# A hybrid trunk layer on one core: where the second block's weights are split and kept, when its rotary tables are asked for, and when the weight sums start

## The chip, the cores and the metric

The kernel runs on one core of a Trainium2 chip. The metric is the device time of one execution in microseconds, as the median of the runs shown.

## What is computed

One layer of a decoder trunk on x of 2048 tokens x 1024 columns, all in f32. Cut to what matters:

```python
h = rmsnorm(x, mix_norm_g)
q, k, v, g, u = split(h @ w_in, 5)                # 512 columns each
y_ret = silu(g) * head_rmsnorm(retention(rope(q), rope(k), v))   # 4 heads of 128
y_pool = pool_mixer(u, pool_w) * pool_scale       # trailing means over 2, 4, 8, 16 tokens
x = x + concat(y_ret, y_pool) @ w_out
x = x + softmax(rmsnorm(x, xa_norm_g) @ wq @ k_mem.T / 16) @ v_mem @ wo   # 256 memory tokens, 4 heads
a = rmsnorm(x, ffn_norm_g) @ w_up                 # 2 x 2816 columns
x = x + (silu(conv3(a)[gate]) * conv3(a)[val]) @ w_down
return rmsnorm(x, final_norm_g)
```

## The kernel before

**Blocks and stages.** The tokens are worked in two blocks of 1024 (`T`; b = 0 and 1), each as two halves of 512 (`SUB`). Block 0 goes through its head inputs and retention, its pools, its out-projection and its attention over the memory; then block 1 does the same. The gated MLP comes last, for both blocks, in rounds.

**Matmuls.** Every f32 product is three passes of 128x512 matmuls on parts of reduced precision: high by high (L268), high by low (L269) and low by high (L270). The high part of an operand is a copy on ScalarE (L1118 for a loaded weight, L258 in `split`), the low part the difference on VectorE (L242).

**Seven products instead of eight.** The MLP, and of block 1 also the projections of q, k, g and u, take a 2x2 block product in the form with seven products, which needs sums of weight quarters and sums of the other operand's quarters. `weight_sums` makes the weights' sums in HBM (`Ad` for the pairs of block 1, `Ud` and `Dd` for the MLP) by software DMAs that GpSimd issues, some copying and some adding. It is a generator: one step is a small copy on ScalarE (L1031) that is held in program order, a copy on GpSimd (L1032) behind it, and up to eight DMAs behind that. Between two steps it yields `spacing[0]` times. `under[0]` is advanced by the units of the out-projections and attention's value product while `slow[0]` is false and `paced[0]` true, and elsewhere by a call in the loop. For `VWd` (attention's last product) `under` is set aside for both blocks.

**The start of block 1.** `values` makes v on PE. Beside it `quarter_sums` loads four pieces of x (j = 0 to 3; `R` and `S` hold them, names from the program's buffers), and writes the sums of quarters as split pairs (G) and, for two kinds, unsplit into `z` (Z). Then `head_projections` runs eight members of seven items each, twelve matmuls an item. An item's weight is loaded by SyncE into one of seven places of 512 columns (`raws`, taken as they come free), split into one of four pairs (`prs`), and read by PE; `fill` runs the splits ahead of PE. `turned_sums` splits what `z` holds, `scaled_tables` asks for the rotary tables (`rope_d`, four DMAs into Z) and multiplies them by the norm's factors (VectorE, L242, Z<-Z,T). Both are advanced by `step` between items.

**What sets the order.** A scheduler orders each engine's instructions from the program's text, its buffers and costs; what stands under `tc.keep_in_program_order` keeps the written order on its engine.

**Attention of block 1.** Sixteen iterations (scores and softmax: L969, L973, L946, L948). Beside them `first_tiles` reads block 1's residual back from HBM (T<-Xd), normalises it (L250), and stores it and its quarter sums (Hd<-T). The MLP's first operands are read from there (T<-Hd, split by L1067 on ScalarE).

Of the kernel before, what the change touches and what calls it, by code (L numbers as in the profile page):

```python
# [11 lines left out]
AF = mybir.ActivationFunctionType  # L12
# [5 lines left out]
KT = D // P  # L18
SEQ = 2048
NMEM = 256  # L20
T = 1024
SUB = 512
# [114 lines left out]
def trunk(ctx, tc, xT, memT, pos, w_qkgu, w_v, wkv, wqT, wo, wout_r, wout_p, poolT, w_up, w_dn, vecs, consts, outT):  # L137
    nc = tc.nc
    pe, act, dve, pool, sp = nc.tensor, nc.scalar, nc.vector, nc.gpsimd, nc.sync
# [17 lines left out]
    def new_s(dtype, at):  # L157
        return cp.tile([P, T], dtype, tag=f"S{at}", name=nm("S"))
# [8 lines left out]
    R = cp.tile([P, 3 * T], F32, tag="R", name="R")  # L167
    Q = cp.tile([P, 3 * T], F32R, tag="Q", name="Q")
    S = [new_s(F32, j) for j in range(2)]
    raws = Places([(R, j * T) for j in range(3)] + [(r, 0) for r in S], T)  # L170
# [70 lines left out]
    def tt(eng, out, a, b, op):  # L241
        return eng.tensor_tensor(out=out, in0=a, in1=b, op=op)  # L242

    def ts(eng, out, a, s1, op0, s2=None, op1=None):
        if op1 is None:
            return eng.tensor_scalar(out=out, in0=a, scalar1=s1, scalar2=None, op0=op0)
        return eng.tensor_scalar(out=out, in0=a, scalar1=s1, scalar2=s2, op0=op0, op1=op1)

    def stt(out, a, s, b, op0=ALU.mult, op1=ALU.add):
        dve.scalar_tensor_tensor(out=out, in0=a, scalar=s, in1=b, op0=op0, op1=op1)  # L250
# [50 lines left out]
    def xpair(k, s):  # L301
        return X[:, 2 * k, s * SUB : (s + 1) * SUB], X[:, 2 * k + 1, s * SUB : (s + 1) * SUB]


    quarter, slow, spacing, paced = [0], [True], [4], [False]
    behind, under, fetched = [iter(())], [iter(())], [None]
# [375 lines left out]
    def pool_group(b, g, rb):  # L682
        out = B.take(2)

        def evac(s, ps):
            u, *bufs = [TT.take() for _ in range(3 if g else 2)]
            tt(dve, u.f[:, 16 : 16 + SUB], ps, rb[s].f[:, :SUB], ALU.mult)
            dve.tensor_copy(u.f[:, 0:16], phalo[:, g])
            dve.tensor_copy(phalo[:, g], u.f[:, SUB : SUB + 16])
            src, lo = u, 1  # L690
            for i in range(g + 1):
                sh = 1 << i
                dst = bufs[i % 2]
                tt(dve, dst.f[:, lo : 16 + SUB], src.f[:, lo : 16 + SUB], src.f[:, lo - sh : 16 + SUB - sh], ALU.add)
                src = dst
                lo += 2 * sh
            cur, d = u.f[:, 16 : 16 + SUB], src.f[:, 16 : 16 + SUB]
            w = 2 << g
            if b == 0 and s == 0:
                tt(dve, d[:, :w], d[:, :w], icnt[:, :w], ALU.mult)  # L700
                ts(dve, d[:, w:], d[:, w:], 1.0 / w, ALU.mult)
                tt(dve, d, d, cur, ALU.subtract)
            else:
                stt(d, d, 1.0 / w, cur, ALU.mult, ALU.subtract)
            split(d, out.r[:, s * SUB : (s + 1) * SUB], out.r[:, T + s * SUB : T + (s + 1) * SUB])
            for r in (u, *bufs):
                r.free()

        unit(load_tile(w_qkgu[12 + g]), xpair, evac)
        return out  # L710
# [388 lines left out]
    class Member:  # L1099
# [15 lines left out]
        def high(self, i, pr):  # L1115
            w = self.n * P
            p2 = pr.r.rearrange("p (i n) -> p i n", i=2)
            act.activation(p2[:, 0, :w], self.raw[i].f[:, :w], AF.Copy)  # L1118
            return p2[:, 0, :w], p2[:, 1, :w]
# [437 lines left out]
        return r.r[:, 2 * j * SUB : (2 * j + 1) * SUB], r.r[:, (2 * j + 1) * SUB : (2 * j + 2) * SUB]  # L1557

    def part_of(z, i, j):
        at = (j // 2) * 2 * T + i * T + (j % 2) * SUB  # L1560
        return z.f[:, at : at + SUB]

    def quarter_sums(b, t1, t2, z):
# [31 lines left out]
    def negated(src, hi, lo):  # L1595
        act.activation(hi, src, AF.Copy, scale=-1.0)
        stt(lo, src, -1.0, hi.bitcast(F32), ALU.mult, ALU.subtract)

    def head_projections(b, v, rb, t1, t2, z):
# [2 lines left out]
        nonlocal raws, prs  # L1602
        pieces, far = B.arenas[0], new_e(F32)
        more = new_s(F32R, 0)
        raws = Places([(R, j * SUB) for j in range(5)] + [(S[1], j * SUB) for j in range(2)], SUB)
        side = Arena(R, 5 * SUB, 1, SUB).take().f
        prs = Places([(Q, j * T) for j in range(3)] + [(more, 0)], T)
        t3 = pieces.take(4)
        todo, ready, mix, gates, outs, tables = [], [], [None] * KT, {}, {}, []

        def place():
            return Z.take() if Z.room() else far.take()

        def turned_sums():
            for j in range(KT // 2):
                split(part_of(z, 0, j), *fourth(t3, j))
                yield
            z.free(0, 1)
            z.free(2, 1)
            for j in range(KT // 2):  # L1620
                negated(part_of(z, 1, j), *xpair(j, 1))
                yield
            z.free(1, 1)
            z.free(3, 1)

        def scaled_tables():
            out = Z.take(2)
            tables.append(out)
            for to, half in ((0, 0), (0, 1), (2, 0), (1, 1)):
                p, i = slice(64 * half, 64 * half + 64), min(to, 1)  # L1630
                sp.dma_start(out.f[p, i * T : (i + 1) * T].rearrange("p (s c) -> p s c", s=NS), rope_d[to].rearrange("(s p) c -> p s c", s=NS))
            yield
            yield
            for i in range(2):
                for s in range(NS):
                    d = out.f[:, i * T + s * SUB : i * T + (s + 1) * SUB]
                    tt(dve, d, d, rb[s].f[:, :SUB], ALU.mult)
                yield
# [37 lines left out]
        class Heads(Member):  # L1676
# [6 lines left out]
            def begun(self):  # L1683
                both_gates = self.groups[0] // 4 == 2
                self.acc = []
                for n in self.groups:
                    if n // 4 == 2:
                        gates[n % 4] = None if both_gates else [TT.take() for _ in range(NS)]
                    if n // 4 == 2 and not both_gates:
                        self.acc.append([g.f[:, :SUB] for g in gates[n % 4]])  # L1690
                    else:
                        r = place()
                        self.acc.append([r.f[:, q * SUB : (q + 1) * SUB] for q in range(NS)])
                        outs[n] = r

            def evac(self, i, ps):
                role, q = ((0, 0), (1, 1), (0, 1), (0, 0), (1, 1), (0, 1), (1, 0))[i]
# [95 lines left out]
            if todo and next(todo[0], True) is not None:  # L1793
                todo.pop(0)

        todo += [turned_sums(), scaled_tables()]
        for at, (m, i) in enumerate(items):
            while len(made) <= at or highs:
                fill()
# [3 lines left out]
            pr = made[at].r.rearrange("p (i n) -> p i n", i=2)  # L1803
# [29 lines left out]
        raws = Places([(R, j * T) for j in range(3)] + [(r, 0) for r in S], T)  # L1833
# [72 lines left out]
    todo = folded_weights()  # L1906

    def folded(n):
        for _ in range(n):
            next(todo, None)  # L1910
# [12 lines left out]
    for b in range(NB):  # L1923

        if b == 0:
            rn, rb, last = normed
            v = values(lambda: rn, wv)
            with tc.issue_after(last.ins):
                tabs = list(rope_tables(0))[-1]
            cs = rope_scale(tabs, rb)  # L1930
            per = [(0, 1, 1), (0, 1, 1), (0, 2, 2), (0, 2, 3)]
            mix = []
            for h in range(HEADS):
                qkg = head_inputs(h, rb, cs, lambda i: folded(per[h][i]))
                mix.append(B.take(2))
                behind[0] = retention(b, h, qkg, v, mix[h])
            folded(100)
            pooled = {g: pool_group(b, g, rb) for g in (0, 3, 2, 1)}
            finish()
            cs.free()  # L1940
            mix += [pooled[g] for g in range(4)]
            mix = [(u, [u.r[:, :T], u.r[:, T:]]) for u in mix]
        else:
            t1, t2 = (B.arenas[0].take(4) for _ in range(2))
            v, z = Z.take(4), Z.take(4)
            more_sums = quarter_sums(b, t1, t2, z)
            next(more_sums)

            def between():
                next(behind[0], None)  # L1950
                if next(more_sums, None) is None:
                    next(under[0], None)

            values(lambda: normed[0], wv, between, v)
            for _ in more_sums:
                pass
            finish()
            rb = normed[1]
            mix = head_projections(b, v, rb, t1, t2, z)
        for r in rb:  # L1960
            r.free()
        slow[0], spacing[0] = False, (4, 4)[b]

        xs = [TT.take() for _ in range(NS)]
        ahead = fetch_x(b, 0)
# [39 lines left out]
                r.free()  # L2005

        beside = tables() if b + 1 < NB else first_tiles(own)
        paced[0], spacing[0] = True, (1, 2)[b]
        prob, behind[0] = attention(xs, beside, b + 1)
        spacing[0] = 3  # L2010
        for _ in beside:
            pass
        under, paused = [iter(())], under
        Z = new_z(F32)
        xs = [TT.take() for _ in range(NS)]
        if b + 1 < NB:
# [45 lines left out]
        under = paused  # L2062
# [28 lines left out]
    raws = Places([(R, j * SUB) for j in range(6)] + [(r, j * SUB) for r in S for j in range(2)], SUB)  # L2091
# [114 lines left out]
```

## Time and profile before

| | before |
|---|---|
| median of 3 runs | 2466.07 us (2465.82 to 2468.02) |
| profiled execution | 2467.87 us, span 2466.1 us |
| mean granted TensorE clock | 0.992 |
| busy PE / VectorE / ScalarE / GpSimd | 2417.9 / 1726.2 / 1288.9 / 316.1 us |
| software DMA queue | 86.00 MB, 14.9% of the 16 DMA engines over the span |

Stages of the profiled execution: block 0 to about 660 us, values of block 1 to 702, pair products to about 925, out-projection to about 1010, attention to 1100 with its value product to 1230, and the MLP from there. Rows of a timeline give start, length, engine, line, operation, tile written <- tiles read, and in brackets how long the engine had been idle and who ended that. PE's durations overlap, since matmuls are pipelined: its pace is read from start to start.

### The profile page before, as it was taken

What the parts mean: (1) busy time and instruction counts of PE and PEld (TensorE: products, weight loads), DVE (VectorE), ACT (ScalarE), POOL (GpSimd) and SP (SyncE); (2) the same over time, 40 slices, a digit from 0 to 9 for tenths busy, and PEclk for the clock granted to TensorE, in tenths of its full rate; (3) what the DMA queues carried; (4) which work ended last, traced back from release to release, by engine and by line L of the source; (5) the groups of instructions that cost most, each with busy time, mean ns of one, the idle gap of its engine ahead of it and who ended that gap; (6) DMA issues with size and microseconds to landing.
All of it is one profiled execution on the core that took longest, in us unless ns stands there. A gap on an engine that the chain in (4) does not pass through costs nothing.

```text
span 2466.1 us, 33272 instructions
## 1 busy us (share of the span) xinstructions
PE 2417.9 (98%) x11294; PEld 2019.7 (82%) x11294; DVE 1726.2 (70%) x2917; ACT 1288.9 (52%) x2349; POOL 316.1 (13%) x485
## 2 busy tenths in 40 slices
PE   6999999999989999999999999999999999999997
PEld 6888888888878887878888888888888888888886
DVE  8646576564756665565778776886767698867875
ACT  6333423443435554434655655675555577666663
POOL 1000000054255554200000100020000000000000
PEclk9999999999999999999999999999999999999998
DMA  8133524389899999766568664765556478768951
GB/s 292 45 111 111 160 76 136 124 219 324 250 273 274 260 236 321 197 232 213 171 200 270 208 188 151 234 214 162 160 159 216 132 230 307 246 185 283 344 164 69
DMA packets 263595, 502.35 MB, mean 204 GB/s; under 512 B 28800, under 2 KB 57600, under 8 KB 263424
## 3 DMA queue, kind: packets, MB, share of 16 engines
q1 hardware_dynamic: 201536, 385.90, 47.8%
q0 software_dynamic: 37376, 86.00, 14.9%
q10 hardware_dynamic: 24512, 28.32, 3.3%
q8 instruction: 89, 1.46, 0.2%
q14 instruction: 82, 0.67, 0.1%
HBM read 398.65 MB, written 187.43 MB: 238 GB/s over the span
## 4 chain that ended last, share of the span: by engine, by line
PE 93%; DMA 3%; DVE 3%; issue 1%; ACT 0%; SPq 0%; POOL 0%; POOLq 0%; DVEq 0%; ACTq 0%
PE mm L270 29%; PE mm L268 29%; PE mm L269 29%; DMA T<-Xd 1%; PE aux L808 1%; PE aux L824 1%; PE aux L797 1%; PE aux L268 1%; PE aux L269 1%; PE aux L270 1%; PE aux L826 1%; PE aux L349 1%; DMA Z<-rope_d 1%; DMA T<-xT 0%; DVE T L242 0%
## 5 line engine op out<-in xcount | busy, mean ns | idle before, releaser
L268 PE MATMUL mm<-G,Q 128*128 128x512 f32 (+1 forms) x1745 | 673.4, 386 | 19.8 <-ACT Q L258 11.0
L270 PE MATMUL mm<-G,Q 128*128 128x512 f32 (+1 forms) x1745 | 669.9, 385 | 10.5 <-DVE Q L242 10.4
L269 PE MATMUL mm<-G,Q 128*128 128x512 f32 (+1 forms) x1617 | 621.2, 384 | 0.0
L269 PE MATMUL mm<-G,E 128*128 128x512 f32 x1084 | 421.6, 389 | 0.0
L268 PE MATMUL mm<-G,E 128*128 128x512 f32 x1084 | 420.1, 390 | 0.0
L270 PE MATMUL mm<-G,E 128*128 128x512 f32 x1084 | 419.2, 389 | 0.0
L268 PEld LDWEIGHTS mm<-G,Q 128*128 128x128 f32 x1745 | 332.0, 190 | 84.8 <-ACT Q L258 12.4
L270 PEld LDWEIGHTS mm<-G,Q 128*128 128x128 f32 x1745 | 331.5, 190 | 76.0 <-DVE Q L242 13.2
L269 PEld LDWEIGHTS mm<-G,Q 128*128 128x128 f32 x1617 | 308.0, 191 | 57.1
L242 DVE TENSOR_TENSOR Z<-Z,mm 128x512 f32<-128x512 f32 x296 | 201.4, 681 | 111.7 <-PE mm L270 104.7
L250 DVE SCALAR_TENSOR_TENSOR Z<-Z,vecs 128x1024 f32<-128x1024 f32 x176 | 224.5, 1279 | 50.2 <-ACT Z L1181 45.5
L270 PEld LDWEIGHTS mm<-G,E 128*128 128x128 f32 x1084 | 203.5, 188 | 42.4
L269 PEld LDWEIGHTS mm<-G,E 128*128 128x128 f32 x1084 | 203.5, 188 | 42.2
L268 PEld LDWEIGHTS mm<-G,E 128*128 128x128 f32 x1084 | 203.5, 188 | 42.1 <-ACT Z L1263 0.2
L1118 ACT ACTIVATE E<-R 128x512 fp32r<-128x512 f32 (+1 forms) x165 | 101.5, 615 | 142.3 <-PE mm L269 135.1
L242 DVE TENSOR_TENSOR T<-T 128x512 f32<-128x512 f32 (+3 forms) x220 | 150.5, 688 | 24.3 <-ACT T L411 15.4
L242 DVE TENSOR_TENSOR G<-T,G 128x512 fp32r<-128x512 f32 (+1 forms) x181 | 119.3, 673 | 44.1 <-ACT G L1067 32.8
L242 DVE TENSOR_TENSOR Q<-R,Q 128x512 fp32r<-128x512 f32 x149 | 103.4, 696 | 66.3 <-ACT Q L258 47.1
L1118 ACT ACTIVATE Q<-R 128x512 fp32r<-128x512 f32 (+1 forms) x153 | 94.5, 618 | 85.4 <-PE mm L269 72.2
L1181 ACT ACTIVATE Z<-Z,vecs 128x1024 f32<-128x1024 f32 x88 | 109.1, 1241 | 36.6 <-DVE Z L242 35.6
L1067 ACT ACTIVATE G<-T 128x512 fp32r<-128x512 f32 x157 | 95.7, 624 | 58.1 <-DMA T<-Hd 27.9
L1118 ACT ACTIVATE E<-S 128x512 fp32r<-128x512 f32 (+1 forms) x107 | 65.8, 616 | 105.0 <-PE mm L269 103.4
(338 smaller groups left out, 3776.7 us busy)
## 6 DMA issues: line engine op xcount, KB each, us to landing
T<-Gd SPq DMA_DIRECT2D x168, 256.0 KB, 4.4
Ud<-w_up POOLq DMA_DIRECT2D x132, 256.0 KB, 10.1
Gd<-Z SPq DMA_DIRECT2D x110, 256.0 KB, 2.7
R<-Ud SPq DMA_DIRECT2D x106, 256.0 KB, 2.8
R<-w_up SPq DMA_DIRECT2D x80, 256.0 KB, 3.1
S<-Ud SPq DMA_DIRECT2D x70, 256.0 KB, 2.9
Gd<-T SPq DMA_DIRECT2D x56, 256.0 KB, 3.3
T<-Xd SPq DMA_DIRECT2D x53, 256.0 KB, 4.6
```

The costliest lines, as they stand in the source:

```text
L242: return eng.tensor_tensor(out=out, in0=a, in1=b, op=op)
L250: dve.scalar_tensor_tensor(out=out, in0=a, scalar=s, in1=b, op0=op0, op1=op1)
L268: pe.matmul(ps, lh, rh, start=start, stop=False, skip_group_check=more)
L269: pe.matmul(ps, lh, rl, start=False, stop=False, skip_group_check=more)
L270: latest[0] = pe.matmul(ps, ll, rh, start=False, stop=stop, skip_group_check=more)
L349: pe.matmul(ps[:, t : t + 1], ap, one, start=True, stop=more is None)
L797: pe.matmul(col(sc, c), self.ch(k, c), self.ch(q, c), start=True, stop=True)
L808: pe.matmul(col(self.kv, c), col(self.kn.f, c), self.ch(v, c, h * T), start=True, stop=True)
L824: pe.matmul(col(y, c), col(self.pr.f, c), self.ch(v, c, h * T), start=True, stop=self.cur[c] is None)
L1067: act.activation(hi, x, AF.Copy)
L1118: act.activation(p2[:, 0, :w], self.raw[i].f[:, :w], AF.Copy)
L1181: act.activation(self.c[g].f, a[:, 2:], AF.Identity, bias=cb[:, f : f + 1], scale=cw[2][:, f : f + 1])
```

## The change

The places for the pairs' weights are listed in the order in which the quarter loads came free (`raws.freed`). `part_of` lays `z` out so that the first kind fills its first two slots and the second kind its last two. `turned_sums` now splits the first kind, frees its two slots, asks for the tables, and only then negates the second kind. `Heads` gets a `high` of its own, which is held in ScalarE's program order. The weight sums are advanced from block 0's pools on, with other spacings, no longer beside the values of block 1, and for block 1 no longer set aside for the value product of attention.

```diff
@@ -1557,7 +1557,7 @@
         return r.r[:, 2 * j * SUB : (2 * j + 1) * SUB], r.r[:, (2 * j + 1) * SUB : (2 * j + 2) * SUB]
 
     def part_of(z, i, j):
-        at = (j // 2) * 2 * T + i * T + (j % 2) * SUB
+        at = i * 2 * T + j * SUB
         return z.f[:, at : at + SUB]
 
     def quarter_sums(b, t1, t2, z):
@@ -1602,7 +1602,9 @@
         nonlocal raws, prs
         pieces, far = B.arenas[0], new_e(F32)
         more = new_s(F32R, 0)
-        raws = Places([(R, j * SUB) for j in range(5)] + [(S[1], j * SUB) for j in range(2)], SUB)
+        rooms = [(R, 0), (R, T), (R, 2 * T), None, (S[1], 0)]
+        rooms = [(rooms[i][0], rooms[i][1] + h * SUB) for i in raws.freed for h in range(1 if i == 2 else 2) if i != 3]
+        raws = Places(rooms, SUB)
         side = Arena(R, 5 * SUB, 1, SUB).take().f
         prs = Places([(Q, j * T) for j in range(3)] + [(more, 0)], T)
         t3 = pieces.take(4)
@@ -1615,13 +1617,8 @@
             for j in range(KT // 2):
                 split(part_of(z, 0, j), *fourth(t3, j))
                 yield
-            z.free(0, 1)
-            z.free(2, 1)
-            for j in range(KT // 2):
-                negated(part_of(z, 1, j), *xpair(j, 1))
-                yield
-            z.free(1, 1)
-            z.free(3, 1)
+            z.free(0, 2)
+            yield from scaled_tables()
 
         def scaled_tables():
             out = Z.take(2)
@@ -1631,6 +1628,10 @@
                 sp.dma_start(out.f[p, i * T : (i + 1) * T].rearrange("p (s c) -> p s c", s=NS), rope_d[to].rearrange("(s p) c -> p s c", s=NS))
             yield
             yield
+            for j in range(KT // 2):
+                negated(part_of(z, 1, j), *xpair(j, 1))
+                yield
+            z.free(2, 2)
             for i in range(2):
                 for s in range(NS):
                     d = out.f[:, i * T + s * SUB : i * T + (s + 1) * SUB]
@@ -1693,6 +1694,11 @@
                         self.acc.append([r.f[:, q * SUB : (q + 1) * SUB] for q in range(NS)])
                         outs[n] = r
 
+            def high(self, i, pr):
+                hi, lo = pr.r[:, :SUB], pr.r[:, SUB:]
+                tc.keep_in_program_order(act.activation(hi, self.raw[i].f, AF.Copy))
+                return hi, lo
+
             def evac(self, i, ps):
                 role, q = ((0, 0), (1, 1), (0, 1), (0, 0), (1, 1), (0, 1), (1, 0))[i]
                 d = self.acc[role][q]
@@ -1793,7 +1799,7 @@
             if todo and next(todo[0], True) is not None:
                 todo.pop(0)
 
-        todo += [turned_sums(), scaled_tables()]
+        todo.append(turned_sums())
         for at, (m, i) in enumerate(items):
             while len(made) <= at or highs:
                 fill()
@@ -1935,6 +1941,7 @@
                 mix.append(B.take(2))
                 behind[0] = retention(b, h, qkg, v, mix[h])
             folded(100)
+            slow[0], paced[0], spacing[0] = False, True, 7
             pooled = {g: pool_group(b, g, rb) for g in (0, 3, 2, 1)}
             finish()
             cs.free()
@@ -1948,8 +1955,7 @@
 
             def between():
                 next(behind[0], None)
-                if next(more_sums, None) is None:
-                    next(under[0], None)
+                next(more_sums, None)
 
             values(lambda: normed[0], wv, between, v)
             for _ in more_sums:
@@ -1959,7 +1965,7 @@
             mix = head_projections(b, v, rb, t1, t2, z)
         for r in rb:
             r.free()
-        slow[0], spacing[0] = False, (4, 4)[b]
+        spacing[0] = (7, 6)[b]
 
         xs = [TT.take() for _ in range(NS)]
         ahead = fetch_x(b, 0)
@@ -2005,12 +2011,12 @@
                 r.free()
 
         beside = tables() if b + 1 < NB else first_tiles(own)
-        paced[0], spacing[0] = True, (1, 2)[b]
+        spacing[0] = (1, 3)[b]
         prob, behind[0] = attention(xs, beside, b + 1)
-        spacing[0] = 3
+        spacing[0] = 6
         for _ in beside:
             pass
-        under, paused = [iter(())], under
+        under, paused = [iter(())] if b == 0 else under, under
         Z = new_z(F32)
         xs = [TT.take() for _ in range(NS)]
         if b + 1 < NB:
```

ScalarE, end of the values stage and start of the pairs. The last two L737 evacuate the last two banks of the values, L1596 and L258 split what `z` holds, L1118 are weights' high parts and L1706 the first evacuation of a pair. Before:

```order
L1118 ACTIVATE Q<-R 128x512
L1596 ACTIVATE G<-Z_4490 128x512
L1031 ACTIVATE halo<-consts 128x2
L258 ACTIVATE G<-Z_4490 128x512
L1596 ACTIVATE G<-Z_4490 128x512
L258 ACTIVATE G<-Z_4490 128x512
L1596 ACTIVATE G<-Z_4490 128x512
L1118 ACTIVATE Q<-R 128x512
L258 ACTIVATE G<-Z_4490 128x512
L737 ACTIVATE Z_4490<-mm_5411,rn_5149 128x4x128
L737 ACTIVATE Z_4490<-mm_5412,rn_5149 128x4x128
L1118 ACTIVATE Q<-S_79 128x512
```

After, where the weights' high parts are L1699 and the evacuation is L1712:

```order
L258 ACTIVATE G<-Z_4550 128x512
L1031 ACTIVATE halo<-consts 128x2
L1596 ACTIVATE G<-Z_4550 128x512
L258 ACTIVATE G<-Z_4550 128x512
L1596 ACTIVATE G<-Z_4550 128x512
L258 ACTIVATE G<-Z_4550 128x512
L737 ACTIVATE Z_4550<-mm_5431,rn_5199 128x4x128
L737 ACTIVATE Z_4550<-mm_5432,rn_5199 128x4x128
L1699 ACTIVATE Q<-R 128x512
L1699 ACTIVATE Q<-S_79 128x512 x2
L1699 ACTIVATE S_5484<-R 128x512
L1712 ACTIVATE E_5483<-mm_5504 128x512
```

Before, high parts stand among the splits and ahead of the values' evacuation; after, all stand behind it. A halo copy (L1031) starts a step of the weight sums: one stands among the splits in either order, but before the change three more stand in the twelve rows ahead of these, and after it none.

VectorE, statistics of the last quarter (`sm`, then `rn`), before:

```order
L242 TENSOR_TENSOR sm_5354<-sm_5352 128x8
L242 TENSOR_TENSOR S_5484<-R,S_5484 128x512
L250 SCALAR_TENSOR_TENSOR sm_5354<-sm_5354,sm_5351 128x8
L250 SCALAR_TENSOR_TENSOR sm_5352<-sm_5354,sm_5352 128x8
L242 TENSOR_TENSOR sm_5354<-sm_5352 128x8
L250 SCALAR_TENSOR_TENSOR sm_5354<-sm_5354,sm_5351 128x8
L250 SCALAR_TENSOR_TENSOR sm_5352<-sm_5354,sm_5352 128x8
L1839 COPY rn_5341<-sm_5352 128x8
```

After:

```order
L242 TENSOR_TENSOR sm_5384<-sm_5382 128x8
L250 SCALAR_TENSOR_TENSOR sm_5384<-sm_5384,sm_5381 128x8
L250 SCALAR_TENSOR_TENSOR sm_5382<-sm_5384,sm_5382 128x8
L242 TENSOR_TENSOR sm_5384<-sm_5382 128x8
L250 SCALAR_TENSOR_TENSOR sm_5384<-sm_5384,sm_5381 128x8
L250 SCALAR_TENSOR_TENSOR sm_5382<-sm_5384,sm_5382 128x8
L1845 COPY rn_5371<-sm_5382 128x8
```

The low part of a weight (S<-R,S) that stood amid the statistics stands there no more.

VectorE, a little later, at the start of the pairs: splits (G<-Z,G), table multiplications (Z<-Z,T) and weights' low parts (Q<-R,Q and the like). Before:

```order
L242 TENSOR_TENSOR G<-Z_4490,G 128x512
L250 SCALAR_TENSOR_TENSOR G<-Z_4490,G 128x512
L242 TENSOR_TENSOR G<-Z_4490,G 128x512
L250 SCALAR_TENSOR_TENSOR G<-Z_4490,G 128x512
L242 TENSOR_TENSOR Q<-R,Q 128x512
L242 TENSOR_TENSOR G<-Z_4490,G 128x512
L242 TENSOR_TENSOR Z_4490<-Z_4490,T 128x512 x4
L242 TENSOR_TENSOR Q<-S_79,Q 128x512
L242 TENSOR_TENSOR Q<-R,Q 128x512
L242 TENSOR_TENSOR E_5483<-E_5483,mm_5576 128x512
L242 TENSOR_TENSOR S_5484<-R,S_5484 128x512
```

After:

```order
L250 SCALAR_TENSOR_TENSOR G<-Z_4550,G 128x512
L242 TENSOR_TENSOR G<-Z_4550,G 128x512
L250 SCALAR_TENSOR_TENSOR G<-Z_4550,G 128x512
L242 TENSOR_TENSOR G<-Z_4550,G 128x512
L242 TENSOR_TENSOR Z_4550<-Z_4550,T 128x512 x2
L242 TENSOR_TENSOR Q<-R,Q 128x512
L242 TENSOR_TENSOR Q<-S_79,Q 128x512 x2
L242 TENSOR_TENSOR Z_4550<-Z_4550,T 128x512 x2
L242 TENSOR_TENSOR S_5484<-R,S_5484 128x512
L242 TENSOR_TENSOR Q<-R,Q 128x512 x2
```

Before, the first low parts stand ahead of all four table multiplications; after, the cosine's two stand ahead of the first low part, and the sine's two ahead of the fourth.

ScalarE, end of block 1's attention. L973 is a softmax, L948 a copy behind PE's score sums, L1067 the split of a tile read back from HBM. Before:

```order
L973 ACTIVATE T,sm_8465<-mm_8439,sm_8464,scl_7830 128x256 x2
L948 ACTIVATE G<-aux_8523 128x4x128
L973 ACTIVATE T,sm_8515<-mm_8489,sm_8514,scl_7830 128x256 x2
L948 ACTIVATE G<-aux_8570 128x4x128
L973 ACTIVATE T,sm_8562<-mm_8536,sm_8561,scl_7830 128x256 x2
L948 ACTIVATE G<-aux_8619 128x4x128
L1067 ACTIVATE G<-T 128x512
L973 ACTIVATE T,sm_8611<-mm_8585,sm_8610,scl_7830 128x256 x2
L948 ACTIVATE G<-aux_8659 128x4x128
L258 ACTIVATE Q<-R 128x512
```

After, the last pieces of the same stretch:

```order
L973 ACTIVATE T,sm_8452<-mm_8426,sm_8451,scl_7730 128x256 x2
L948 ACTIVATE G<-aux_8507 128x4x128
L1031 ACTIVATE halo<-consts 128x2
L973 ACTIVATE T,sm_8499<-mm_8473,sm_8498,scl_7730 128x256 x2
L948 ACTIVATE G<-aux_8566 128x4x128
L973 ACTIVATE T,sm_8558<-mm_8532,sm_8557,scl_7730 128x256 x2
L948 ACTIVATE G<-aux_8606 128x4x128
L258 ACTIVATE Q<-R 128x512
L948 ACTIVATE G<-aux_8625 128x4x128
L1031 ACTIVATE halo<-consts 128x2
L407 ACTIVATE T<-Z_8584 128x512
L1067 ACTIVATE G<-T 128x512
```

L1067 stood ahead of the last L973 and stands behind it now; two halo copies stand among the last softmaxes, where there was none.

## The prediction

> **What bounds the kernel now.** First the page: its line of busy times, and the row of the software DMA queue.
>
> ```profile
> PE 2417.9 (98%) x11294; PEld 2019.7 (82%) x11294; DVE 1726.2 (70%) x2917; ACT 1288.9 (52%) x2349; POOL 316.1 (13%) x485
> ...
> q0 software_dynamic: 37376, 86.00, 14.9%
> ```
>
> PE is the bound: 2417.9 of 2466.1 us. An edit that takes no matmul away can only win back holes in PE's stream. Next, PE's waits (line waited for; us in total, times, longest) and the busy time by stage (the fields after the length are PE, PEld, DVE, ACT and POOL; the last three are granted clock, DMA share and GB/s).
>
> ```profile
> PE mm L270 <- DVE Q L242: 10.4, 8, 4.0
> ...
> PE mm L268 <- ACT Q L1118: 3.8, 2, 2.8
> ...
> PE aux L946 <- DVE T L246: 1.7, 1, 1.7
> ```
>
> ```profile
> 340.00:460.00 120.00, 120.00 (x560) 100.32 (x559) 78.07 (x161) 37.84 (x76) 0.00 (x0) 1.00 0.34 108
> ...
> 500.00:600.00 100.00, 100.00 (x467) 82.49 (x466) 53.87 (x117) 43.37 (x104) 51.75 (x85) 1.00 1.01 272
> ...
> 702.00:730.00 28.00, 21.63 (x74) 17.18 (x75) 15.93 (x27) 9.12 (x18) 14.23 (x24) 0.82 1.07 310
> ...
> 880.00:950.00 70.00, 65.89 (x328) 53.42 (x327) 47.09 (x105) 32.16 (x83) 36.32 (x56) 1.00 0.97 258
> ...
> 1055.00:1110.00 55.00, 53.28 (x252) 43.79 (x251) 37.40 (x77) 17.30 (x44) 0.00 (x0) 1.00 0.72 247
> ```
>
> Three stages that the diff touches have holes: 702 to 730 us, where block 1's pair products begin, with 28.00 - 21.63 = 6.4 us idle and the clock down to 0.82; 880 to 950 with 4.1 us idle; and 1055 to 1110 with 1.7 us. The rest of the holes lies in the kernel's first and last stages, which the diff leaves alone. Now PE's timeline at the holes.
>
> ```profile
> 697.79 0.39 PE L270 MATMUL mm<-E,G 128*128 128x512 f32 x1
> ...
> 701.19 0.39 PE L270 MATMUL mm<-E,G 128*128 128x512 f32 x1
> 704.34 0.68 PE L268 MATMUL mm<-G,Q 128*128 128x512 f32 x1 [2.76 <-ACT Q L1118]
> ...
> 718.90 0.80 PE L270 MATMUL mm<-G,Q 128*128 128x512 f32 x1 [4.03 <-DVE Q L242]
> ...
> 1101.63 0.63 PE L946 MATMUL aux<-consts,T 128*128 128x128 f32 x4 [1.72 <-DVE T L246]
> ```
>
> From 697.79 to 701.19 PE starts a matmul 15 times, 3.40 / 15 = 0.227 us each. The 74 matmuls of 702 to 730 need 74 x 0.227 = 16.8 us of the 28.0, so 11.2 us are lost there, and with the first 0.4 us of the hole that opens at 701.6, 11.6: 6.8 in the two waits, 4.8 at half clock after them. The chain of waits says why (start, length, what):
>
> ```profile
> 682.93 8.47 DMA R<-w_qkgu
> ...
> 704.57 12.36 DMA Z<-rope_d
> ```
>
> **The pairs' start.** On VectorE, an item's low part stands in the middle of the last quarter's statistics, and waits for a weight whose load was issued at 682.93:
>
> ```profile
> 692.17 0.69 DVE L242 TENSOR_TENSOR S<-R,S 128x512 fp32r<-128x512 f32 x1 [5.87 <-ACT S L1118]
> ...
> 696.67 0.69 DVE L250 SCALAR_TENSOR_TENSOR G<-R,G 128x512 fp32r<-128x512 f32 x1
> ...
> 714.83 1.29 DVE L242 TENSOR_TENSOR Z<-Z,T 128x512 f32<-128x512 f32 x2 [8.69 <-DMA Z<-rope_d]
> ```
>
> The edit hands the first items the places whose quarters were read first, and in the new order that low part has left the spot. So the 5.87 us wait goes and the quarter's sums end at 697.4 - 5.7 = 691.7 (I keep 0.2 back for the handover). The weights of items 1 to 4 are loaded into places freed still earlier. Next the table request on SyncE, and ScalarE's last steps before the pairs:
>
> ```profile
> 702.55 2.66 SPq L1631 DMA_DIRECT2D Z<-rope_d  x4
> ```
>
> ```profile
> 703.65 0.63 ACT L1118 ACTIVATE Q<-R 128x512 fp32r<-128x512 f32 x1
> ...
> 704.71 1.24 ACT L737 ACTIVATE Z<-mm,rn 128x512 f32<-128x512 f32 x2
> ```
>
> The request hangs on the same quarter, so the first two of its DMAs move from 702.55 to about 702.55 - 5.7 = 696.9; the seven item loads ahead of it on SyncE have their places by 691.7. Two prices are new.
>
> First, the pinned high part. It now stands behind both L737 on ScalarE, and the second of those needs PE's last values matmul, which ends at 701.6. So PE must wait for L737 and the high part: 1.24 / 2 + 0.63 = 1.25, with handovers 1.35 us. Nothing covers that. Bounds: 0.7 (the high part slips in front after all) to 2.8 (as now).
>
> Second, low part 0 now stands behind the two cosine multiplications on VectorE, so a late table holds PE. How late depends on what else the DMA engines carry:
>
> ```profile
> q0 software_dynamic: 1642, 3.97, 65.3%
> ...
> R<-Ad SPq DMA_DIRECT2D x5, 256.0 KB, 7.3
> ...
> Z<-rope_d SPq DMA_DIRECT2D x4, 256.0 KB, 10.3
> ```
>
> ```profile
> R<-Ud SPq DMA_DIRECT2D x106, 256.0 KB, 2.8
> ```
>
> From 695 to 720 the weight sums held 65.3% of the engines' time, and a table took 10.3 us (median) from issue to landing; loads of the same size elsewhere take 2.8 (the page's median over 106). After the change the values stage starts no step of the sums, and ScalarE's order has one halo copy, which starts a step, near the turned splits where it had four. I take the middle, 6.5: landed at 703.4. Two multiplications and the low part follow, 1.29 + 0.69 = 2.0, so 705.4. PE starts at 701.6 + 1.35 = 702.9, does four matmuls with high parts (0.9) and wants the low part at 703.8: 1.6 us of waiting, from 0 (tables in 2.8) to 5.4 (10.3 again).
>
> The clock: it was halved after the 2.76 us wait and after the 4.03, and not after the 1.72 (1.00 in the row of 1055 to 1110). Two waits of 1.35 and 1.6 with 0.9 of work between lie in the middle; I put half a chance on one stretch of half clock costing 1.7, so 0.85. The Trainium skill ("TensorE: Matmul & The Clock Gate", Part 1) lets the clock fall only after an idle window of about 3.4 us; this trace differs, since 2.76 us was enough. By its rule the 0.85 would be 0 and the gain here 8.65.
>
> Sum here: 11.6 lost now, 1.35 + 1.6 + 0.85 = 3.8 lost then: **-7.8 us**, between -10.9 (0.7 and nothing else) and about 0 (2.8, 5.4 and two stretches of half clock).
>
> **The weight sums, earlier and thinner.** 14.9% of 2466.1 is 367 us of all 16 engines, in 45 steps (one for each halo copy of POOL):
>
> ```profile
> L1032 POOL COPY halo<-halo 128x2 f32<-128x2 f32 x45 | 33.5, 744 | 547.3 <-ACT halo L1031 547.3
> ```
>
> So a step is worth 8.2 us of the engines. Seven of them now fall into block 0's pools and out-projection. There PE has no hole (120.00 of 120.00) with a DMA share of 0.34, and it has none from 500 to 600 either, at a share of 1.01 with a step every few matmuls. I charge **+0.5**, bounds 0 and +3. Block 1's products and out-projection get fewer steps for each product, so the waits of 880 to 950 can only find the DMAs faster; but the order there changes as well: **-1**, bounds -4 and +2.
>
> **Attention of block 1.** Here steps are new: before, POOL does nothing from 1055 to 1110. PE's score sums come one iteration apart:
>
> ```profile
> 1055.88 0.60 PE L946 MATMUL aux<-consts,T 128*128 128x128 f32 x4
> 1061.82 0.38 PE L946 MATMUL aux<-consts,T 128*128 128x128 f32 x2
> ```
>
> One step stands in every three iterations of ScalarE's new order, 17.8 us, so the sums take 8.2 / 17.8 = 46% of the engines, beside a chain of loads and stores that feeds VectorE just in time:
>
> ```profile
> Hd<-T SPq DMA_DIRECT2D x23, 256.0 KB, 2.8
> T<-Xd SPq DMA_DIRECT2D x12, 256.0 KB, 3.8
> ```
>
> ```profile
> 1089.68 2.90 DMA T<-Xd
> ...
> 1095.85 0.69 DVE sm L969
> ...
> 1097.17 2.56 DMA Hd<-T
> 1099.73 1.17 ACT T L973 x4
> ```
>
> ```profile
> 1099.17 0.63 ACT L1067 ACTIVATE G<-T 128x512 fp32r<-128x512 f32 x1 [6.43 <-DMA T<-Hd]
> ```
>
> Now the last softmax (L973) stands behind L1067, which waits for a tile's way out to HBM and back; the new order puts every L973 ahead of it, and that reason for the 1.72 us goes. Against it, a load that meets a running step takes 6.8 or so instead of 3.8 (the 7.3 and 10.3 above were under 65%). PE would not have waited with L973 at 1099.7 - 1.7 = 1098.0, and VectorE's last reduction (L969) ended at 1096.5, so about 1.5 us of lateness is free: one load that is 3 late costs 1.5, two 4.5, one that takes 10.3 costs 5. Taking between one and two, 3.2 less 1.7: **+1.5**, bounds -1.7 and +7.
>
> **Sum.** -7.8 + 0.5 - 1 + 1.5 = -6.8 us against the profiled execution's 2467.9: 2461.1. The median of the runs shown, 2466.07, lies 1.8 below that execution, so the forecast for the median is 2459.3. A measurement of this kernel tells some 0.2%, 4.9 us, from no change.
>
> **Rivals.**
> (a) *The tables come as late as now.* For: VectorE's new row makes PE's low part wait for them, and four transfers of 256 KB follow seven loads and a step of sums. Against: they are asked for 5.7 us earlier. At 10.3 they land at 707.2, the low part is ready at 709.2, PE waits 5.4, and the half clock costs another 3.4: 1.35 + 5.4 + 3.4 = 10.2 of 11.6 lost again. With the other terms -1.4 - 1 + 2 = -0.4: about 2465.7.
> (b) *Slower: attention of block 1 starves.* A step beside each of the last two quarters' loads, each 6.5 late (10.3 for 3.8), is 13 late, less 1.5 free: 11.5 us of PE, and 3.4 of half clock after so long a wait; less 1.7 that went. That is +13.2 - 7.8 + 0.5 - 1 = +4.9, 2471. It decides from about 8 us of lateness in that chain, where it eats the pairs' gain. For: the loads have no slack to speak of. The Trainium skill ("DMA: Bandwidth & Descriptors", "Issuing engines are not separate DMA queues") says the same for any engine that issues: all transfers share the 16 DMA engines and interleave; the 10.3 against 2.8 above agrees. Against: only every second load meets a step.
> (c) *Nearly everything at the pairs is won.* Tables in 2.8 us: no second wait, no half clock, -10.2; attention without lateness, -1.7; out-projection -1: 2453.
>
> **Chances.** Forecast (2456 to 2462.5) 0.50, of it 0.38 below 2461.1 and 0.12 above; (a) 0.18, within 0.2%; (b) 0.16, slower; (c) 0.16, faster. Faster 0.54, within 0.2% 0.30, slower 0.16. The range leaves out (b) and the lower part of (c): 2453 to 2469, whose upper end takes in (a) with 3 us of attention.
>
> **What would show it.** In the changed profile: no idle of some 5.9 us on VectorE near 686; the tables requested near 697 and landed by 704; PE's first pair matmul at about 703 and its next wait under 2 us, with at most one stretch of half clock; 702 to 730 with some 108 matmuls; L1067 behind the last L973, and the wait on L946 under 4 us. I am wrong if the tables land after 707, if PE waits for the high part of a later item because ScalarE is held in program order by a late load, or if the loads of block 1's attention run over by more than 5 us.

## The result, and the profile after

| | before | after |
|---|---|---|
| median | 2466.56 us (4 runs, 2465.82 to 2468.02) | 2485.77 us (4 runs, 2481.55 to 2488.60) |
| profiled execution | 2467.87 us | 2487.77 us |

The ratio is 1.0073, with a 95% interval of 1.0061 to 1.0086: 19 us slower, where 6.8 us faster was forecast and the range ended at 2469. Four more runs of the same kernel, made beside the experiments, gave 2485.76 us.

PE's waits in the profile after (line waited for; us in total, times, longest):

```profile
PE mm L268 <- ACT Q L258: 11.7, 6, 8.9
PE mm L270 <- DVE Q L242: 10.5, 8, 2.3
PE aux L946 <- DVE T L246: 5.9, 2, 3.1
...
PE mm L268 <- ACT Q L1118: 3.6, 1, 3.6
...
PE mm L268 <- ACT E L258: 3.0, 1, 3.0
PE mm L268 <- ACT Q L1699: 1.7, 2, 1.3
PE mm L268 <- ACT Z L1712: 1.5, 2, 1.3
```

Busy time by stage (PE, PEld, DVE, ACT, POOL; then granted clock, DMA share, GB/s). Before, in two stages that the prediction does not show:

```profile
730.00:880.00 150.00, 149.97 (x778) 127.86 (x777) 103.08 (x200) 79.44 (x191) 82.64 (x125) 1.00 1.05 268
...
1110.00:1230.00 120.00, 120.00 (x539) 99.59 (x539) 72.14 (x107) 62.96 (x104) 1.94 (x8) 1.00 0.57 187
```

After:

```profile
702.00:730.00 28.00, 24.36 (x99) 19.20 (x98) 18.90 (x33) 10.71 (x18) 1.78 (x4) 0.94 0.64 187
730.00:880.00 150.00, 146.70 (x753) 122.48 (x752) 98.24 (x194) 74.81 (x180) 40.89 (x64) 1.00 0.67 174
880.00:950.00 70.00, 63.41 (x307) 51.21 (x306) 43.05 (x97) 29.01 (x74) 25.38 (x35) 0.95 0.81 212
...
1055.00:1110.00 55.00, 49.07 (x211) 39.72 (x211) 32.42 (x69) 14.97 (x43) 17.23 (x27) 0.91 0.82 237
1110.00:1230.00 120.00, 116.24 (x508) 94.86 (x507) 64.40 (x105) 53.93 (x104) 34.42 (x51) 0.99 1.01 315
```

The first row has 99 matmuls where before had 74: the pairs' start did get better. Every other stage shown got worse: PE idles 3.3 us in the pairs (0.0 before), 6.6 from 880 to 950 us (4.1), 5.9 in attention (1.7) with the clock at 0.91 for 1.00, and 3.8 in attention's value product (0.0). PE's timeline has the places:

```profile
704.36 0.50 PE L268 MATMUL mm<-G,Q 128*128 128x512 f32 x1 [1.29 <-ACT Q L1699]
707.96 0.50 PE L270 MATMUL mm<-G,Q 128*128 128x512 f32 x1 [2.35 <-DVE Q L242]
799.79 0.50 PE L270 MATMUL mm<-G,Q 128*128 128x512 f32 x1 [1.14 <-DVE Q L242]
...
876.93 0.50 PE L268 MATMUL mm<-G,Q 128*128 128x512 f32 x1 [1.28 <-ACT Z L1712]
...
930.99 1.65 PE L268 MATMUL mm<-E,Q 128*128 128x512 f32 x3 [3.04 <-ACT E L258]
...
1088.69 1.09 PE L946 MATMUL aux<-consts,T 128*128 128x128 f32 x4 [3.13 <-DVE T L246]
...
1100.44 0.63 PE L946 MATMUL aux<-consts,T 128*128 128x128 f32 x4 [2.80 <-DVE T L246]
...
1201.00 0.79 PE L268 MATMUL mm<-G,Q 128*128 128x512 f32 x1 [3.59 <-ACT Q L1118]
```

Idle time and half clock are seen together when the starts of the matmul of the same number (PE runs 11294 in both) are compared between two profiled executions. In the table each number says how many us later than before a kernel starts the 3620th matmul (751 us in before, the pairs), the 4560th (933 us, start of the out-projection), the 5400th (1118 us, attention done), the 5800th (1209 us, the MLP's first operands are wanted) and the last. Some 0.5 to 2.5 us of each row arise in the first 230 us, whose code no kernel here changes. Each row is one execution, and a kernel's runs differ among themselves, by 5 us in pin_start and by 12 in quiet_end_dense; so the rows say where time goes, and the medians below how much.

| kernel | 751 | 933 | 1118 | 1209 | last |
|---|---|---|---|---|---|
| after | -4.4 | +5.1 | +15.2 | +20.6 | +19.9 |
| after, once more | -4.5 | +4.9 | +14.7 | +19.0 | +18.7 |
| no_pin | -10.2 | -8.6 | -0.2 | +4.2 | +2.8 |
| sums_only | -10.8 | -9.7 | -2.2 | +2.5 | +1.3 |
| pairs_only | -5.9 | +6.0 | +9.4 | +9.4 | +8.8 |
| pin_only | -6.7 | +6.9 | +5.6 | +5.6 | +5.5 |
| pin_start | -4.1 | -2.1 | +5.5 | +10.0 | +9.3 |
| places_tables | -8.6 | -8.3 | -9.0 | -9.0 | -9.1 |
| values_quiet | -9.5 | -8.1 | -2.0 | -2.0 | -2.5 |
| attn_quiet | -3.5 | +6.0 | +9.4 | +14.3 | +13.3 |
| dense3 | -3.1 | +10.8 | +9.6 | +9.6 | +8.2 |
| quiet_end | -10.4 | -7.9 | -7.9 | -7.9 | -9.4 |
| quiet_end_dense | -4.9 | -2.8 | -3.9 | -3.9 | -4.5 |
| quiet_end_pin | -5.2 | +5.3 | +3.4 | +3.4 | +1.9 |
| quiet_end_only | -9.2 | -7.6 | -4.8 | -4.8 | -5.2 |

### The profile page after: what moved, and what is told of

The parts are those of the page before. It is cut to its first block, busy times and chain, and to the rows that moved or that the text cites. A ratio compares the mean times of both kernels' runs of the same rounds, so it can differ in the third digit from the quotient of the medians.

```text
span 2486.0 us, 33306 instructions
## 1 busy us (share of the span) xinstructions
PE 2426.3 (98%) x11294; PEld 2022.1 (81%) x11294; DVE 1726.2 (69%) x2917; ACT 1288.2 (52%) x2349; POOL 323.0 (13%) x485
## 4 chain that ended last, share of the span: by engine, by line
PE 88%; DMA 6%; DVE 3%; ACT 1%; issue 1%; POOLq 0%; SPq 0%; POOL 0%; ACTq 0%; DVEq 0%
PE mm L268 28%; PE mm L270 28%; PE mm L269 27%; DMA T<-Hd 2%; DMA T<-Xd 1%; DMA Z<-xT 1%; DVE T L242 1%; DVE Q L242 1%; PE aux L797 1%; DMA Z<-Xd 1%; DVE Z L242 1%; DVE G L242 1%; PE aux L349 1%; PE aux L270 1%; PE aux L268 1%
## 5 line engine op out<-in xcount | busy, mean ns | idle before, releaser
L270 PE MATMUL mm<-G,Q 128*128 128x512 f32 (+1 forms) x1745 | 670.3, 386 | 10.7 <-DVE Q L242 10.5
L1118 ACT ACTIVATE E<-R 128x512 fp32r<-128x512 f32 (+1 forms) x165 | 101.4, 615 | 139.5 <-PE mm L269 131.4
L1032 POOL COPY halo<-halo 128x2 f32<-128x2 f32 x45 | 29.0, 645 | 839.9 <-ACT halo L1031 839.9
L1067 ACT ACTIVATE G<-T 128x512 fp32r<-128x512 f32 x157 | 96.0, 625 | 61.1 <-DMA T<-Hd 32.0
L1118 ACT ACTIVATE E<-S 128x512 fp32r<-128x512 f32 (+1 forms) x107 | 65.9, 616 | 106.2 <-PE mm L269 101.1
```

Source lines behind the costliest of these rows:

```text
L270: latest[0] = pe.matmul(ps, ll, rh, start=False, stop=stop, skip_group_check=more)
L1032: turn = pool.tensor_copy(there, here)
L1067: act.activation(hi, x, AF.Copy)
```

## The experiments

Theory 1 says that the sums' DMAs slow the loads beside them, wherever they are put; theory 2 (rival A in the first expectations) that the pin of the high parts makes the waits from 780 to 931 us. Medians and intervals are against before on the same chip.

### The two halves of the change

**pairs_only** takes the sums' schedule back and keeps the rest.

```diff
-            slow[0], paced[0], spacing[0] = False, True, 7
-                next(more_sums, None)
+                if next(more_sums, None) is None:
+                    next(under[0], None)
-        spacing[0] = (7, 6)[b]
+        slow[0], spacing[0] = False, (4, 4)[b]
-        spacing[0] = (1, 3)[b]
+        paced[0], spacing[0] = True, (1, 2)[b]
-        spacing[0] = 6
+        spacing[0] = 3
-        under, paused = [iter(())] if b == 0 else under, under
+        under, paused = [iter(())], under
```

> The pairs' part of the change alone (places by age, layout of z, tables sooner, pinned high parts); the weight sums run as before. Theory 1 (the sums' DMAs make the loss): the 6.8 us won at the pairs' start stay and the loss behind 1055 us goes: about 2460, 6 to 7 us under before. Rival A (the pin makes the waits between 780 and 930 us): PE's waits there stay, some 5 to 11 us, and the time is 2465 to 2471. If the start's gain needs the quieter DMAs (four steps of sums run beside the tables again), the start loses up to 10 us as before and the time is 2466 or above.

2473.11 us, 1.0027 (1.0015 to 1.0039). Slower than before with no step in attention: theory 1 alone fails. It is also slower than rival A's 2465 to 2471. Between 751 and 933 us it loses 11.9 us, more than after does there (9.5).

**sums_only** does the reverse: before, with the six lines above as after has them.

> The new schedule of the weight sums alone on the kernel before. Theory 1: attention of block 1 and its value product lose some 15 us to slow loads (T<-Xd of 9 us, T<-Hd of 13): 2480 to 2486 with the pairs' start as before or a few us better for the quieter DMAs. Rival A: the losses after 1055 us are the same, but no waits between 780 and 880 us.

2470.13 us, 1.0014 (1.0005 to 1.0024), far under the 2480 expected. Two things come apart. In attention and behind it the kernel loses 12.2 us (from -9.7 to +2.5), as theory 1 said. But at 751 us it is 10.8 us *ahead*, without places, tables or pin, and PE has no hole there:

```profile
702.00:730.00 28.00, 28.00 (x123) 22.69 (x123) 19.03 (x33) 11.79 (x20) 4.14 (x9) 1.00 0.64 179
```

### The pin

**no_pin** is after without `Heads.high`.

```diff
-            def high(self, i, pr):
-                hi, lo = pr.r[:, :SUB], pr.r[:, SUB:]
-                tc.keep_in_program_order(act.activation(hi, self.raw[i].f, AF.Copy))
-                return hi, lo
```

> The changed kernel without the pin of the weights' high parts in ScalarE's program order. Rival A: the waits near 800 and 877 us go (3 us) and what hangs on them, so 2475 to 2482. Theory 1 alone: within noise of the changed kernel, 2482 to 2488.

2470.52 us, 1.0013 (1.0003 to 1.0023): 15 us under after, twice what was expected. 5.8 of it is won at the start (-10.2 for -4.4), another 7.9 between 751 and 933 us (+1.6 for +9.5).

**pin_only** puts the same method into before and changes nothing else.

> The kernel before with the weights' high parts held in ScalarE's program order, and nothing else. If the pin alone makes the waits at 800, 877 and 918 to 931 us (theory 2), this is some 10 to 15 us slower than before: 2476 to 2482. If the pin only hurts together with the new places or tables, it stays within 4 us of before.

2475.62 us, 1.0026 (1.0016 to 1.0037). From 751 to 933 us it loses 13.6 us. At the start it gains 6.7: the pin, too, takes the low part out of the last quarter's statistics. So three separate edits (the sums' schedule, places with tables, the pin) each mend the start; the pin takes more than that back from 751 to 933 us, the schedule in attention and behind it, and only places with tables (below) keep their lead.

**pin_start** pins the first member's seven high parts only.

```diff
-                tc.keep_in_program_order(act.activation(hi, self.raw[i].f, AF.Copy))
+                copy = act.activation(hi, self.raw[i].f, AF.Copy)
+                if self.groups == PAIRS[0]:
+                    tc.keep_in_program_order(copy)
```

> The changed kernel with the pin on the first member's seven high parts only. Theory 2: the waits of 1.3 and 2.4 us at the pairs' start stay (some 5 us with the clock), and the later ones (800, 877, 918 to 931 us) go: about 9 us less than the changed kernel, 2475 to 2479. If a late wait comes from the delayed start itself, it stays and the time is 2482 or above.

2478.78 us, 1.0050 (1.0035 to 1.0065), 7.0 us under after. The start is as in after (-4.1), the loss to 933 us is 2.0 instead of 9.5. The later pins cause the later loss; a delayed start does not.

What the later pins do is seen in ScalarE's waits from 730 to 930 us, here with the rows of the rotary copies (L1728 in after, L1723 in no_pin). L803 is a copy behind PE's transposes. After:

```profile
ACT T L803 <- PE aux L799: 15.9, 6, 6.6
ACT R L1728 <- DVE Z L242: 15.2, 8, 2.6
...
ACT R L1728 <- DVE E L242: 3.1, 2, 2.2
```

No pin:

```profile
ACT Q L1118 <- PE mm L269: 24.2, 16, 2.2
ACT T L803 <- PE aux L799: 7.4, 3, 2.9
...
ACT R L1723 <- DVE E L242: 5.6, 4, 2.2
...
ACT R L1723 <- DVE Z L242: 3.5, 5, 1.4
```

At the rotary copies ScalarE waits for VectorE 18.3 us in after and 9.1 in no_pin, in about as many waits (10 and 9).

`final` turns a finished quarter of q or k through one buffer, `side`: ScalarE copies the halves into it (L1728), VectorE multiplies and adds, and the next copy must wait until VectorE is done. ScalarE's rows run one behind the other. With the pin, a high part stands behind such a copy, an evacuation (L1712) behind that, and PE waits for the evacuation, as ScalarE's timeline of after shows at 873 us (the last rows left out are eight short copies of L830, 1.0 us):

```profile
869.51 1.28 ACT L1728 ACTIVATE R<-E 64x512 f32<-64x512 f32 x2 [2.17 <-DVE E L242]
870.82 0.63 ACT L1699 ACTIVATE Q<-S 128x512 fp32r<-128x512 f32 x1
...
873.42 1.28 ACT L1728 ACTIVATE R<-E 64x512 f32<-64x512 f32 x2 [0.94 <-DVE E L242]
874.73 0.63 ACT L1699 ACTIVATE S<-S 128x512 fp32r<-128x512 f32 x1
...
876.27 0.61 ACT L1712 ACTIVATE Z<-mm 128x512 f32<-128x512 f32 x1
```

The evacuation ends at 876.9, where PE's 1.28 us wait ends. Only this wait was followed to its source; that the others of this stretch, 3.04 at 930.99 among them, come by the same way is not shown. The pin also changes PE's own order: the tiles of its matmuls, in order, differ from before in 589 of 11294 places in after and in 34 in no_pin. That the pin makes the loss is shown by taking it out and putting it in; by which of these ways is in part argued. Without the pin the scheduler had put the high parts ahead, where their wait was for PE (24.2 us of L1118 above), that is, they were early.

### Places and tables

**places_tables** is pairs_only without the pin: places by age, z's layout, tables sooner, sums as before.

> The pairs' part of the change without the pin (places by age, layout of z, tables sooner), with the weight sums as before. If the places and the tables do what they were forecast to, they alone win 7 to 11 us at the pairs' start even beside the sums: 2456 to 2460. If only quieter DMAs win there, 2464 to 2468.

2463.16 us, 0.9981 (0.9971 to 0.9990). PE's two waits at the start shrink to one, though the sums hold 80.3% of the DMA engines there:

```profile
715.66 0.50 PE L270 MATMUL mm<-G,Q 128*128 128x512 f32 x1 [1.21 <-DVE Q L242]
```

```profile
q0 software_dynamic: 2128, 4.92, 80.3%
...
Z<-rope_d SPq DMA_DIRECT2D x4, 256.0 KB, 7.4
```

At the start these edits do what was forecast of them: 8.6 us ahead at 751 us in its profiled execution. But that execution, at 2458.76 us, was the shortest of ten, and the median misses the 2456 to 2460 expected: 4.7 us are left. The granted clock, on record for every run, goes the same way: 0.995 in this execution and 0.993 as the median of the other nine. If the missing share is time at half clock, those 0.002 are worth some 5 us of 2457 (an estimate, from rounded values).

### The sums' traffic

**values_quiet** is before with one edit: no steps beside block 1's values.

```diff
-                if next(more_sums, None) is None:
-                    next(under[0], None)
+                next(more_sums, None)
```

> The kernel before with the weight sums left out of the loop beside the values of block 1 alone (the steps come later). If the start of the pairs lost its 11.6 us to the sums' DMAs (theory 1), PE has no wait between 702 and 730 us and the lead is about 11 us there; four steps then fall into block 1's attention and may take 2 to 6 back: 2456 to 2464. If the places by age are what is needed, the waits of 2.8 and 4.0 us stay and it is 2466 or more.

2465.91 us, 0.9996 (0.9987 to 1.0006), above the 2464 expected. At 751 us it is 9.5 us ahead; the steps left over fall into attention, where 6.1 go again. The tables were asked for at 699.97 us (702.55 before) and took 8.2 us (median) for 10.3, and PE did not wait. How much of that is the earlier request and how much the faster landing is not separated.

**attn_quiet** is after with `under[0]` put aside during block 1's attention.

```diff
         spacing[0] = (1, 3)[b]
+        held = under[0]
+        if b:
+            under[0] = iter(())
...
+        under[0] = held
```

> The changed kernel with no step of the weight sums during block 1's attention: the steps that stood there run later, beside attention's value product and the start of the MLP. Theory 1: the two waits of 3 us on score sums (near 1089 and 1100 us) go and some 10 us with them, but the loads of the MLP's first operands (T<-Hd) are then as slow or slower, so the 5 us near 1201 us stay or grow: 2476 to 2482, against some 2486 for the changed kernel. If the attention's loss came from elsewhere, 2484 to 2488.

2476.33 us, 1.0042 (1.0027 to 1.0057). From 933 to 1118 us it loses 3.4 us for after's 10.1, and at the value product 4.9 for 5.4: without steps most of attention's loss goes, and where they still run, the loss stays. The 3.4 that is left stands in pairs_only too, which has no step there either. The table's row is of this kernel's slowest run (2481.22 us).

**dense3** is after with spacing 4 in block 0's pools and both out-projections and 3 in block 1's pairs, so that the last step stands ahead of block 1's attention.

> The changed kernel with the sums' steps closer together (spacing 4 in block 0's pools and both out-projections, 3 in block 1's pairs), so that all 45 steps stand ahead of block 1's attention. Theory 1: attention of block 1 and its value product lose nothing, 15 us less than the changed kernel: about 2471, and less if the waits at 780 to 930 us also came from the sums. If the loss there is not the sums' DMAs but the order, the time stays at 2482 to 2488.

2478.98 us, 1.0048 (1.0033 to 1.0063), where 2471 was expected. Nothing is lost from 933 to 1209 us, but block 0 pays: PE waits 1.89 us for its attention's score sums, up to 491 us (L946 again), and from 751 to 933 us it loses 13.9 us with the pin beside denser sums (quiet_end_dense, the same without the pin, loses 2.1).

The loads show how. Before, from 1055 to 1100 us, T<-Xd took 3.8 us, with no software DMA; after, with the sums at 39.6% of the DMA engines:

```profile
q0 software_dynamic: 1792, 4.00, 39.6%
...
Hd<-T SPq DMA_DIRECT2D x18, 256.0 KB, 4.4
...
T<-Xd SPq DMA_DIRECT2D x9, 256.0 KB, 7.7
```

From 1100 to 1190 us, T<-Hd before and, below it, after:

```profile
T<-Hd SPq DMA_DIRECT2D x26, 256.0 KB, 4.4
```

```profile
q0 software_dynamic: 4780, 11.05, 50.5%
...
T<-Hd SPq DMA_DIRECT2D x17, 256.0 KB, 13.3
```

And the chain of waits of after strings them together:

```profile
1064.59 9.01 DMA T<-Xd
...
1078.43 4.62 DMA Hd<-T
1083.11 9.89 DMA T<-Xd
...
1103.84 6.99 DMA T<-Xd
...
1119.47 14.14 DMA Z<-Xd
1133.63 14.14 DMA T<-Hd
...
1181.14 13.31 DMA T<-Hd
```

### Both causes taken away

**quiet_end** is after without the pin, with spacing 7 (block 0) and 4 (block 1) in the out-projections and 3 in the pairs, block 0's pools as in after.

```diff
-            def high(self, i, pr):
...
-        spacing[0] = (7, 6)[b]
+        spacing[0] = (7, 4)[b]
-        spacing[0] = 6
+        spacing[0] = 3
```

> The changed kernel without the pin, and with the sums' spacing 3 in block 1's pairs and 4 in its out-projection, so that the last step stands ahead of block 1's attention; the rest as changed. Theory 1 and 2 together: nothing lost at the pairs' start (11 us under before there), nothing in attention: 2455 to 2460. If the sums' traffic in the pairs costs as much as it did in attention, 2466.

2458.47 us, 0.9965 (0.9954 to 0.9976): faster than both kernels. PE's lead of 10.4 us at 751 us is still 7.9 at 1209. Once more (**quiet_end_again**), 2460.31 us, 0.9974 (0.9963 to 0.9985).

> Places, tables and that schedule without the pin, once more beside the other two: 2457 to 2460.

PE's waits in quiet_end. Of after's waits on L946 (two, 5.9 us) and L1118 (one, 3.6) short ones are left, and none is on a pair's evacuation (L1707 here) any more:

```profile
PE mm L270 <- DVE Q L242: 6.3, 5, 2.1
...
PE aux L946 <- DVE T L246: 1.3, 1, 1.3
PE mm L268 <- ACT E L258: 1.3, 1, 1.3
PE mm L268 <- ACT Q L1118: 1.2, 1, 1.2
```

**quiet_end_dense** has spacing 4 in block 0's pools and out-projection too.

> The same with spacing 4 in block 0's pools and out-projection as well. Theory 1 and 2: as the last one, less some 2 to 4 us lost near 490 us, where the denser sums of the third experiment's sort made PE wait 1.9 us for block 0's attention: 2457 to 2463.

2464.79 us, 0.9986 (0.9974 to 0.9997), above the 2457 to 2463 expected and 6.3 us slower than quiet_end on the same chip. PE waits 2.84 us, up to 493 us, for block 0's score sums: block 0's out-projection and attention bear steps at spacing 7, not at 4.

**quiet_end_pin** puts the pin back, and **quiet_end_only** has that schedule without pin, places and tables.

> The changed kernel, pin included, with the last step of the weight sums ahead of block 1's attention (spacing 3 in block 1's pairs, 4 in its out-projection). Theory 2: nothing is left that the sums take, so what is slower than the same kernel without the pin (2458.5) is the pin's price, 12 to 15 us, all of it between 703 and 940 us: 2470 to 2474. If the pin's price came from meeting the sums' traffic behind it, 2460 to 2464.

> The kernel before with that schedule of the weight sums alone: no pin, no places by age, no sooner tables. If places and tables win nothing once the sums are out of the values stage, this is as fast as with them, 2457 to 2460. If they still win something, it is 2461 or above.

With the pin 2469.87 us, 1.0016 (1.0007 to 1.0026): 9.6 us over quiet_end_again on the same chip, just under the 2470 to 2474 expected. The profiled execution loses 10.5 us between 751 and 933 us, and the waits at 799, 876 and 930 us are back (1.14, 1.36, 3.18). The pin costs that with no step of the sums in attention behind it. The schedule alone gives 2461.99 us, 0.9976 (0.9967 to 0.9986), 1.7 us above quiet_end_again; the intervals overlap, so what places and tables add once the sums have left the values stage is not settled.

## Why the prediction was wrong

- **The pairs' start** (forecast -7.8): the mechanism and the size held. PE is 4.4 us ahead at 751 us, some 6 when the 1.5 us of the first 230 are left out. The first wait was 1.29 for 1.35, the second 2.35 for 1.6 (the tables landed in 6.8 us, median, for 6.5), and one stretch of half clock followed, which the forecast had at half a chance (0.94 over 28 us is 3.4 us at half, 1.7 lost). But the forecast took "the places" as the cause; values_quiet shows that keeping the sums out of the values stage is enough by itself. And without the pin neither wait is left (no_pin is 5.8 us further ahead), so with the sums out of the way both waits of the new start hang on the pin.
- **The step that failed first: "Nothing covers that. Bounds: 0.7 ... to 2.8".** The pin was priced at the first item only, and at nothing for the others. It holds for all 56 items. Measured: 9.5 us from 751 to 933 us in after, where PE waits 8.5 us for 3.6 before, and half clock takes some 3.4 (0.95 from 880 to 950 us, 1.00 before); 1.2 of the 9.5 are in neither. Without the pin the waits are 3.6 us again, as before, and the 1.6 that no_pin still loses there is clock (0.97 from 880 to 933 us for 1.00). The prediction's last sentence named a late load as what could hold ScalarE; in the wait that was followed it was VectorE, through the one buffer `side`.
- **"The waits of 880 to 950 can only find the DMAs faster"** (-1): they grew, the longest from 1.27 to 3.04 us. In no_pin it is 1.27 again, with the same sums; the pin makes it, not the DMAs. How far each late evacuation carries on to it was not measured.
- **Attention of block 1** (+1.5, up to +7): +10.1 from 933 to 1118 us. The share was right (46% estimated, 39.6% measured), the load's price near (6.8 for 7.7), but the count was wrong: one to two late loads were priced, and the median of nine was late. The chain shows T<-Xd at 9.01 and 9.89 us, where before's has 2.9 to 5.8; PE waited 3.13 and 2.80 us, and the clock fell to 0.91. L1067 ran behind the last softmax as said; what that is worth can't be seen beside the larger waits. Rival (b), that this stage starves, was the nearest, and gave 2471.
- **Not priced at all: the steps after attention.** The diff's `under` for block 1 puts them beside the loads of the MLP's first operands. T<-Hd took 13.3 us, and PE lost 5.4 us at 1201.
- **Block 0** (+0.5): nothing was lost at spacing 7 (the lag stays at 1.5 us from 230 us to the end of the values); dense3 and quiet_end_dense show what 4 costs.

The forecast's -7.8 became about -6, and +9.5, +10.1 and +5.4 were added to it: +19, as the medians have it.

## What to carry to other kernels

A pin in program order is priced over every instruction it holds, against the longest wait that any neighbour on that engine can have, and not at the place that it was made for. Background transfers have no free place while a chain of loads feeds the engines just in time: before moving them, read for every stage how late its loads may be, and let the last of them end ahead of the tightest one. When a change has several parts that each mend the same hole, try them singly: here one line of the schedule (values_quiet) did at the pairs' start what the other parts did there together.

## What was not expected of the hardware

- Loads of 256 KB took 7.7 us for 3.8 with the software queue at 39.6% of the DMA engines, and 13.3 for 4.4 at 50.5%. The queue's share alone does not set the delay: in places_tables it was 80.3%, and the tables' loads of the same size took 7.4. The Trainium skill ("DMA: Bandwidth & Descriptors", "Issuing engines are not separate DMA queues") has all issuers' transfers interleave on the same engines; the trace agrees, in that loads beside the sums took longer.
- The clock fell after two short waits of 1.29 and 2.35 us with 1.3 us of matmuls between them (0.94 in that window), and it did not after 1.30 and 0.68 in pin_only nor after a single 1.21 in places_tables (1.00 in both). Half clock shows in PE's pace: behind the 3.59 us wait at 1201 us after's matmuls start some 0.43 us apart, for 0.23 in full. The Trainium skill ("TensorE: Matmul & The Clock Gate", Part 1) asks for an idle window of about 3.4 us; here less was enough. But the length of the waits does not decide it alone. After 1.29 and 0.63 us in pairs_only the clock fell too (0.94), and the same 3.6 us of short waits between 870 and 930 us left it at 1.00 in before and took it to 0.97 in no_pin. What decides was not measured.
